# A hybrid decoder layer on one core: two small matmul runs of a key head put into one run on four array quarters, and all scores of a query block put into one run

## The chip, the cores and the metric

The kernel runs on one core of one Trainium2 chip. The metric is the device time of one execution in microseconds (us), given as the median over runs. TensorE (PE) does the matmuls, VectorE (DVE) and ScalarE (ACT) the elementwise work, GpSimd (POOL) the masks, and SyncE (SP) issues nearly all DMAs from one queue, in order.

## The reference, cut to what matters

One decoder layer over 512 tokens of width 2048 in float32. A normalised input is multiplied by one wide matrix (`w_in`); its columns feed two branches. One is sliding-window attention with 32 query heads over 4 key/value heads. The other is a gated delta rule with 16 key heads, each serving two value heads. Both are projected, gated, summed and projected again.

```
# attention, per block of 128 queries, two blocks of 128 keys in view
s = jnp.einsum('bnqhgd,bnkhd->bnhgqk', qb, kb) * (SWA_HEAD_DIM ** -0.5)
...
# delta rule, per chunk of 64 tokens
L = jnp.where(strict, jnp.einsum('bhncd,bhnsd->bhncs', k_beta, k) * decay, 0.0)
t_inv = lax.linalg.triangular_solve(eye + L, ...)
u = t_inv @ v_beta
w = t_inv @ (k_beta * jnp.exp(g)[..., None])
```

The kernel joins two chunks of 64 into one of 128. The inverse of the joined 128x128 lower triangular block is made of the two 64x64 inverses T1 and T2 and of an off-diagonal block, which is T2 times the block of L between the chunks times T1. These are the two "block products" of the title: the first multiplies the block between the chunks with T1 (its result is called `Y`), the second multiplies `Y` with T2. Both work on 64x64 matrices, for two value heads and four chunk pairs in each key head: eight matmuls each, which the profile counts as 16, since a plain float32 matmul is recorded as two.

## The kernel before, in words

Nearly all PE time goes into large products. `channel_tile` makes one tile of 128 channels by 512 tokens out of 16 steps over the 2048 inputs. Each step is three matmuls of 128x128 by 128x512 (`mm3`, lines 273 to 275), since weights and activations are split into a high and a low part: weights by ACT (`whi`, line 61) and DVE (`wlo`, line 62), half a tile at a time, into a ring of three halves. So one half serves 24 matmuls.

All the small work of the branches is written as Python generators. After every second step `channel_tile` calls `pump`, which lets each live generator go on if the number of pumps that it yielded has passed. One pump is thus six large matmuls. A generator's `yield 2` leaves 12 of them on PE between the code ahead of it and the code behind it. The tile framework then orders the instructions of each engine; it can move an instruction by a few places, and PE executes in the resulting order. PE is never left without work by intent: the small matmuls stand in the stream of large ones.

The stages follow one another: start and key heads (`delta_keys`), attention (about 540 to 1014 us), delta heads (about 1014 to 2130 us), and the output projections.

In the delta heads, `heads(wk, g)` runs for g = 0 to 15: a query tile, two value tiles and two gate tiles. `queries` loads what `keys` and `solve` left in DRAM: `ta` (T1), `lab` (the block between the chunks), `ts1` and the tiles `TT` (T2 and the full inverse to be completed). Then come, two pumps apart, `pqk`, the first block product `py` (line 955) with its copy `Y` (line 957), and the second block product `pu` (lines 961 and 962), which DVE multiplies into `TT` (line 964). The scan over the four chunk pairs reads `TT` afterwards. A 64x64 matmul uses a quarter of the array: the half of the rows that its operands' partitions name and the half of the columns that its output's partitions name. `py` uses two quarters, low rows into high columns and high rows into low columns; `pu` uses two as well, low and high rows, both into the low columns.

In attention, `group` runs for n = 0 to 3 (a key/value head with its eight query heads), and `attend` goes over four query blocks. A block's scores are made in two parts (`pp` = 0 and 1, four heads each): matmuls `S` (line 1461 in block 0, line 1466 in the others, on all four quarters), eviction by ACT (line 1473) or DVE (lines 1475, 1479), maxima (line 1484), `yield 2`. Then follow softmax, transposes `pP` and products `O` (line 1529). `scales` of the next group (`qss`, `pss`) falls into a group's last block.

PSUM has eight banks. In attention the pools hold 2 (large products), 2 (`ptp`), 3 (`psS`, the scores) and 1 (`psO`, the output `O`). In the delta heads they hold 2, 3 (`ptp`) and 3 (the scan).

Of the kernel before, what the change touches and what calls it, by code (L numbers as in the profile page):

```python
# [7 lines left out]
F32 = mybir.dt.float32  # L8
# [5 lines left out]
PSUM = bass.MemoryType.PSUM  # L14
DRAM = bass.MemoryType.DRAM

P = 128
# [3 lines left out]
NTB = T // P  # L21
EPS = 1e-6
KH = 16
VH = 32
QH = 32
HD = 64
# [19 lines left out]
class Layer:  # L46
# [653 lines left out]
    def delta_heads(self):  # L700
        tc, nc = self.tc, self.nc
        with ExitStack() as sb:
            self.ptp = sb.enter_context(tc.tile_pool(name="ptph", bufs=3, space=PSUM, reuse_waits="tile"))
            self.psc = sb.enter_context(tc.tile_pool(name="psch", bufs=3, space=PSUM, reuse_waits="tile"))
            self.gwk = sb.enter_context(tc.tile_pool(name="gwkh", bufs=1, reuse_waits="tile"))
            wk = sb.enter_context(tc.tile_pool(name="dnB", bufs=2, reuse_waits="tile"))
            self.tt = []
            for n in range(4):
                t = wk.tile([P, NTB, P], F32, tag=f"tt{n}", name=f"tt{n}", bufs=1)
                nc.gpsimd.memset(t[HD:P, :, 0:HD], 0.0)  # L710
                self.tt.append(t)
            while not self.solved:
                self.step_slow(self.solves)
            ws = sb.enter_context(tc.tile_pool(name="wsum", bufs=1, reuse_waits="tile"))
            sums = None
            for g in range(KH):
                if g == 3:
                    sums = self.paced(self.weight_sums(ws), 2.0)
                if g == 8:
                    self.drain_slow(self.solves)  # L720
                self.heads(wk, g)
            for j in range(9, 12):
                self.merge_gate("ma", j, self.ma_d)
            self.drain_live()
            self.drain_slow(sums)
# [83 lines left out]
    def solve(self, wk, b, eng):  # L809
# [48 lines left out]
        for k2 in range(2):  # L858
# [2 lines left out]
                out=self.ts_d[b, k2].rearrange("h c j i -> (h c) (j i)"), in_=A[s].rearrange("u j i -> u (j i)")  # L861
            )

    def heads(self, wk, g):

        st = {"z": []}
        self.go(self.queries(wk, g, self.channel_tile(f"q{g}"), st), 0)
        for e in range(2):
            self.go(self.values(wk, g, e, self.channel_tile(f"v{2 * g + e}"), st), 0)
        for e in range(2):  # L870
            self.go(self.zgate(wk, self.channel_tile(f"z{2 * g + e}"), st), 0)
# [23 lines left out]
    def queries(self, wk, g, ps, st):  # L895

        nc = self.nc
        sl = lambda c: slice(c * P, (c + 1) * P)
        q = wk.tile([P, T], F32, tag="y", name="yq", bufs=3)
        yield from self.conv(wk, ps, g, q)  # L900
        M = [self.decay_load(wk, 2 * g + e) for e in range(2)]
        kT = wk.tile([P, T], F32, tag="kT", name="kT")
        nc.sync.dma_start(out=kT, in_=self.kT_d[g])
        yield 2
        pt = self.ptp.tile([P, T], F32, tag="tp", name="ptq")
        self.transpose4(pt, lambda c: q[:, sl(c)])
        ss = self.sumsq(wk, pt)
        yield 3
        epsq = wk.tile([P, NTB], F32, tag="epsq", name="epsq")
        nc.vector.tensor_scalar(out=epsq, in0=ss, scalar1=EPS, scalar2=EPS * P, op0=ALU.add, op1=ALU.mult)  # L910
        yield 1
        for e in range(2):
            self.decay_mask(M[e])
        masks = self.last_mask
        ta = wk.tile([P, NTB, HD], F32, tag="ta", name="ta", bufs=1)
        lab = wk.tile([P, NTB, HD], F32, tag="lab", name="lab", bufs=1)
        ts1 = wk.tile([P, NTB, HD], F32, tag="ts1", name="ts1", bufs=1)
        qd, TT = [], []
        for e in range(2):
            h = 2 * g + e  # L920
            qe = wk.tile([P, NTB, P], F32, tag="qe", name="qe", bufs=2)
            nc.sync.dma_start(out=qe.rearrange("p c i -> p (c i)"), in_=self.eg_rows[h].partition_broadcast(P))
            qd.append(qe)
            b, hl = h // 16, h % 16
            t = self.tt[h % 4]
            for k2 in range(2):
                s = slice(k2 * HD, (k2 + 1) * HD)
                nc.sync.dma_start(out=t[s, :, s], in_=self.ts_d[b, k2, hl].rearrange("c j i -> j c i"))
            s = slice(e * HD, (e + 1) * HD)
            nc.sync.dma_start(out=ta[s], in_=self.ta_d[b, hl].rearrange("c i j -> i c j"))  # L930
            nc.sync.dma_start(out=lab[s], in_=self.lab_d[h])
            if e:
                nc.sync.dma_start(out=ts1[0:HD], in_=self.ts_d[b, 1, hl].rearrange("c j i -> j c i"))
            TT.append(t)
        yield 3
        for e in range(2):
            self.decay_exp(M[e], 2 * g + e)
        k = wk.tile([P, NTB, P], F32, tag="k", name="k")
        nc.sync.dma_start(out=k.rearrange("p c d -> p (c d)"), in_=self.k_d[g])
        yield 1  # L940
        for e in range(2):
            qf = qd[e].rearrange("p c i -> p (c i)")
            self.behind(nc.gpsimd.tensor_tensor(out=qf, in0=qf, in1=q, op=ALU.mult), masks)  # L943
        yield 1
        pqk = self.ptp.tile([P, NTB, P], F32, tag="tp", name="pqk")
        for c in range(NTB):
            nc.tensor.matmul(pqk[:, c, :], lhsT=kT[:, sl(c)], rhs=q[:, sl(c)], start=True, stop=True)
        for e in range(2):
            nc.vector.tensor_tensor(out=M[e], in0=pqk, in1=M[e], op=ALU.mult)
        yield 2  # L950
        py = self.ptp.tile([P, NTB, HD], F32, tag="tp", name="py")
        own = [slice(0, HD), slice(HD, P)]
        for c in range(NTB):
            for e in range(2):
                nc.tensor.matmul(py[own[1 - e], c, :], lhsT=lab[own[e], c, :], rhs=ta[own[e], c, :], start=True, stop=True)
        Y = wk.tile([P, NTB, HD], F32, tag="Y", name="Y", bufs=1)
        nc.vector.tensor_copy(out=Y, in_=py)
        yield 2
        pu = [self.ptp.tile([P, NTB, HD], F32, tag="tp", name="pu") for _ in range(2)]
        for c in range(NTB):  # L960
            nc.tensor.matmul(pu[0][0:HD, c, :], lhsT=Y[HD:P, c, :], rhs=TT[0][HD:P, c, HD:P], start=True, stop=True)
            nc.tensor.matmul(pu[1][0:HD, c, :], lhsT=Y[0:HD, c, :], rhs=ts1[0:HD, c, :], start=True, stop=True)
        for e in range(2):
            nc.vector.tensor_tensor(
                out=TT[e][0:HD, :, HD:P],
                in0=pu[e][0:HD],
                in1=self.neg_beta[0:HD, :, 2 * g + e].unsqueeze(2).to_broadcast([HD, NTB, HD]),
                op=ALU.mult,
            )
        yield 2  # L970
        while "v1" not in st:
            yield 1
        yield 2
        yield from self.scan(wk, g, k, kT, TT, qd, M, epsq, st)
# [338 lines left out]
    def attention(self):  # L1313
        tc, nc, a = self.tc, self.nc, self.a
        with ExitStack() as es:
            self.ptp = es.enter_context(tc.tile_pool(name="ptpa", bufs=2, space=PSUM, reuse_waits="tile"))
            self.psS = es.enter_context(tc.tile_pool(name="pS", bufs=3, space=PSUM, reuse_waits="tile"))
            self.gwk = es.enter_context(tc.tile_pool(name="gwka", bufs=1, reuse_waits="tile"))
            self.psO = es.enter_context(tc.tile_pool(name="pO", bufs=1, space=PSUM, reuse_waits="tile"))
            keep = es.enter_context(tc.tile_pool(name="akeep", bufs=1, reuse_waits="tile"))  # L1320
            self.vtok_a = keep.tile([P, NTB, 256], F32, name="vtok_a")
            self.vdiff = []
# [10 lines left out]
            blk = keep.tile([P, P], F32, name="blk")  # L1333
# [17 lines left out]
            wk = es.enter_context(tc.tile_pool(name="awk", bufs=2, reuse_waits="tile"))  # L1351
# [89 lines left out]
    def attend(self, wk, kd, n, mask, sink, qs, rs, sg, done):  # L1441
        nc = self.nc
        for i in range(NTB):
# [1 line left out]
            isl = slice(i * P, (i + 1) * P)  # L1445
            r = rs[:, i, :]
            mx = wk.tile([P, 8], F32, tag="mx", name="mx")
            sm = {}
            for pp in range(2):
                tl = []  # L1450
                for e in range(2):
                    ps = self.psS.tile([P, 2, 2 * P], F32, tag="S", name="S")
                    t = wk.tile([P, 4, P], F32, tag="sm", name="sm", bufs=5)[:, 0:2, :]
                    tl.append((ps, t))
                for j in range(2):
                    for e, (ps, t) in enumerate(tl):
                        b = slice(e * HD, (e + 1) * HD)
# [5 lines left out]
                        for u in range(2):  # L1463
# [3 lines left out]
                                ps[rr, j, HD - o : 256 - o], lhsT=q[b, i * P + o : i * P + o + HD],  # L1467
                                rhs=kd[b, (i - 1) * P + o : (i - 1) * P + o + 192], start=True, stop=True,
                            )
                wide = [P, 2, P]  # L1470
                for e, (ps, t) in enumerate(tl):
                    if i:
                        nc.scalar.copy(out=t, in_=ps[:, :, HD : HD + P])
# [46 lines left out]
                    else:  # L1520
                        nc.vector.tensor_copy(out=pT, in_=pt)
            yield 3 if i else 2
            po = self.psO.tile([P, 4, P], F32, tag="O", name="O")
            h = n % 2 * HD
            own = self.vtok_a[:, i, n * HD : (n + 1) * HD]
            for kb in kbs:
# [295 lines left out]
```

## Time and profile before

| | |
|---|---|
| median of 3 runs | 2826.55 us (2824.06 to 2827.06) |
| profiled execution | 2822.3 us, its span 2820.5 us |
| PE busy | 2790.0 us (99% of the span) |
| DVE busy | 1947.0 us (69%) |
| ACT busy | 1207.8 us (43%) |
| granted TensorE clock | 0.999 |
| attention, 540 to 1014 us | PE 472.84, DVE 340.12, ACT 214.01 us |
| delta heads, 1014 to 2130 us | PE 1111.11, DVE 735.00, ACT 451.95 us |

PE is busy nearly throughout, so a stretch of PE's time that goes away comes off the total unless another engine then makes PE wait. The ends of matmuls are modelled in the profile; what a small run costs is best read from the starts of the large matmuls around it.

### The profile page before, as it was taken

Reading aid. Unit: us, or ns where it says so; the run is one execution under the profiler, and the core shown is the slowest. Engines: PE = TensorE matmul, PEld = TensorE weight load, DVE = VectorE, ACT = ScalarE, POOL = GpSimd, SP = SyncE. Lnnn points to the kernel's source line nnn. Section 1 sums busy time; section 2 is a strip of 40 time slices with the busy share of each in tenths; the row PEclk is TensorE's granted clock in tenths of the full one; section 3 lists DMA queues with packets and bytes.
Section 4 is the critical chain, followed back from the end, with each engine's and each line's share of the span. In section 5 each row is a group of like instructions: output and inputs, shape, how many; then the busy total and the mean of one; then the engine's idle time right before and its main releaser. Section 6 shows DMA issues by size and latency. Waiting matters only on the chain.

```text
span 2820.5 us, 38292 instructions
## 1 busy us (share of the span) xinstructions
PE 2790.0 (99%) x14090; PEld 2271.8 (81%) x14090; DVE 1947.0 (69%) x3237; ACT 1207.8 (43%) x2508; POOL 145.1 (5%) x124
## 2 busy tenths in 40 slices
PE   8999999999999999999999999999999999999999
PEld 5788888877777788888888888888888788888887
DVE  7866976877758667687676666666657766664666
ACT  5554443244544434334543434434335454432443
POOL 0010110100000010000000000000000000000000
PEclk9999999999999999999999999999999999999999
DMA  9878763323262253366786666676657887885684
GB/s 403 350 241 250 257 226 129 111 79 105 74 172 92 90 183 116 113 222 228 251 262 236 225 234 245 223 241 218 228 184 243 298 301 243 300 270 186 245 313 170
DMA packets 228992, 603.38 MB, mean 214 GB/s; under 512 B 76706, under 2 KB 103074, under 8 KB 188482
## 3 DMA queue, kind: packets, MB, share of 16 engines
q1 hardware_dynamic: 228804, 600.93, 62.3%
q8 instruction: 111, 1.82, 0.3%
q14 instruction: 77, 0.63, 0.1%
HBM read 480.38 MB, written 118.24 MB: 212 GB/s over the span
## 4 chain that ended last, share of the span: by engine, by line
PE 90%; DMA 4%; DVE 3%; ACT 1%; issue 1%; SPq 0%; POOL 0%; DVEq 0%; POOLq 0%; ACTq 0%
PE mm L273 22%; PE mm L275 22%; PE mm L274 21%; PE m L274 4%; PE m L275 4%; PE m L273 4%; PE pv L996 1%; PE pod L1015 1%; PE O L1529 1%; DMA E<-g_rows 1%; PE pod L1014 1%; PE pod L1011 1%; PE pp L986 1%; PE S L1466 1%; DVE wlo L62 1%
## 5 line engine op out<-in xcount | busy, mean ns | idle before, releaser
L273 PE MATMUL mm<-hh,whi 128*128 128x512 f32 x2784 | 1127.7, 405 | 0.1
L275 PE MATMUL mm<-hh,wlo 128*128 128x512 f32 x2784 | 1088.7, 391 | 0.0
L274 PE MATMUL mm<-hl,whi 128*128 128x512 f32 x2784 | 1086.8, 390 | 0.0
L62 DVE TENSOR_TENSOR wlo<-raw,whi 128x1024 fp32r<-128x1024 f32 x516 | 634.8, 1232 | 413.4 <-ACT whi L61 403.7
L61 ACT CAST whi<-raw 128x1024 fp32r<-128x1024 f32 x516 | 540.8, 1049 | 830.2 <-PE mm L274 590.3
L273 PEld LDWEIGHTS mm<-hh,whi 128*128 128x128 f32 x2784 | 523.3, 188 | 116.8 <-issue 14.3
L275 PEld LDWEIGHTS mm<-hh,wlo 128*128 128x128 f32 x2784 | 522.5, 188 | 113.4 <-DVE wlo L62 0.3
L274 PEld LDWEIGHTS mm<-hl,whi 128*128 128x128 f32 x2784 | 524.0, 188 | 101.2 <-issue 1.4
L1261 DVE TENSOR_TENSOR q<-q,q 128x1024 f32<-128x1024 f32 x96 | 123.5, 1286 | 0.0
L807 ACT ACTIVATE E<-E,neg_g 128x128 f32<-128x128 f32 x256 | 81.0, 390 | 82.3 <-POOL E L801 80.4
L837 DVE TENSOR_TENSOR atmp<-A 128x62 f32<-128x62 f32 (+30 forms) x124 | 109.0, 879 | 0.5
L845 DVE TENSOR_TENSOR A<-A,atmp 128x62 f32<-128x62 f32 (+30 forms) x124 | 106.9, 862 | 0.5
L943 POOL TENSOR_TENSOR qe<-qe,yq 128x512 f32<-128x512 f32 x32 | 51.8, 1636 | 931.6 <-DMA qe<-eg_rows 624.2
L1016 ACT COPY osb<-pod 128x256 f32<-128x256 f32 x64 | 23.8, 372 | 153.4 <-PE pod L1015 153.4
L801 POOL TENSOR_SCALAR_AFFINE_SELECT E<-E 128x512 f32<-128x512 f32 x64 | 63.3, 1002 | 416.3 <-DMA E<-g_rows 344.2
L998 ACT COPY vn<-pv 128x256 f32<-128x256 f32 x64 | 23.9, 373 | 115.2 <-PE pv L996 115.2
L652 DVE SCALAR_TENSOR_TENSOR yv<-mm,convh,yv 128x511 f32<-128x511 f32 (+2 forms) x96 | 71.3, 743 | 1.1
L1497 ACT ACTIVATE sm<-sm,mx,rs 128x128 f32<-128x128 f32 x128 | 61.5, 482 | 2.4 <-DVE nbet L828 0.7
L1003 DVE TENSOR_SCALAR vs<-vn,kd 128x128 f32<-128x128 f32 x96 | 23.2, 284 | 54.3 <-ACT vn L998 54.3
L472 DVE SCALAR_TENSOR_TENSOR wa<-wa,silu_cb 128x2048 f32<-128x2048 f32 x22 | 50.2, 2287 | 3.7 <-DMA wa<-in_w_ada_ss 3.7
L1026 DVE SCALAR_TENSOR_TENSOR S<-S,egl,pod 128x128 f32<-128x128 f32 x64 | 19.2, 342 | 47.9 <-ACT junk L1019 47.9
L657 ACT ACTIVATE th<-yv 128x512 f32<-128x512 f32 x32 | 20.1, 629 | 65.4 <-DVE yv L652 65.4
(448 smaller groups left out, 3660.1 us busy)
## 6 DMA issues: line engine op xcount, KB each, us to landing
raw<-in_w_ch SPq DMA_DIRECT2D x158, 1024.0 KB
wa<-in_w_ada_ss SPq DMA_DIRECT2D x32, 1024.0 KB
q<-in_w_od SPq DMA_DIRECT2D x64, 512.0 KB
g_d<-q SPq DMA_DIRECT2D x64, 512.0 KB
raw<-g_d SPq DMA_DIRECT2D x32, 1024.0 KB
raw<-in_w_od SPq DMA_DIRECT2D x24, 1024.0 KB
gw<-in_w_ada_gate SPq DMA_DIRECT2D x16, 1024.0 KB
E<-g_rows SPq DMA_DIRECT2D x64, 256.0 KB
```

The costliest lines, as they stand in the source:

```text
L61: h = self.nc.scalar.copy(out=hi, in_=src)
L62: l = self.nc.vector.tensor_tensor(out=lo, in0=src, in1=hi.bitcast(F32), op=ALU.subtract)
L273: nc.tensor.matmul(ps, lhsT=wh, rhs=xh, start=first, stop=False)
L274: nc.tensor.matmul(ps, lhsT=wh, rhs=xl, start=False, stop=False)
L275: self.last_mm = nc.tensor.matmul(ps, lhsT=wl, rhs=xh, start=False, stop=last)
L652: nc.vector.scalar_tensor_tensor(out=y[:, s:], in0=ps[:, : T - s], scalar=w[:, j : j + 1], in1=y[:, s:], op0=ALU.mult, op1=ALU.add)
L801: self.last_mask = self.nc.gpsimd.affine_select(out=E, in_=E, pattern=[[0, NTB], [1, P]], compare_op=ALU.is_ge, fill=NEG, base=0, channel_ ...
L807: self.nc.scalar.activation(E[:, c, :], E[:, c, :], AF.Exp, bias=self.neg_g[:, c, h : h + 1])
L837: eng.tensor_tensor(out=t, in0=A[:, m : m + 1, m + 1 :].to_broadcast([P, m, n]), in1=A[:, :m, m : m + 1].to_broadcast([P, m, n]), op=ALU.mult,
L845: self.behind(eng.tensor_tensor(out=A[:, :m, m + 1 :], in0=A[:, :m, m + 1 :], in1=t, op=ALU.add))
L1261: self.behind(nc.vector.tensor_tensor(out=q[f], in0=q[x], in1=q[y], op=ALU.add))
L1497: nc.scalar.activation(t, t, AF.Exp, scale=r[:, h : h + 1], bias=mx[:, h : h + 1], accum_out=den[:, h : h + 1])
```

## The change

In the delta heads, the first block product of key head g+1 is now made in the run of the second block product of key head g. It writes the upper partitions of the two `pu` banks, so that the run uses all four quarters: `pu` of g the low columns, the first product of g+1 the high columns. `Y` is then copied by DVE in two pieces and waits for a whole key head until it is read. `ta` and `lab` are loaded one key head ahead, behind the loads of `TT` and `ts1`. For g = 0 a generator of its own (`first_blocks`) loads them and makes the first product six pumps into the stage. The inverses of the second half of the heads are now asked for at g = 7 instead of 8.

In attention, both parts' score matmuls stand ahead of the evictions, so that there are 16 matmuls in a row (8 in block 0) in place of twice 8 (twice 4). The scores get a fourth PSUM bank; the bank of `O` is given up and `O` takes turns with `pP`, `qss` and `pss` in `ptp`.

```
-                if g == 8:
+                if g == 7:
                     self.drain_slow(self.solves)
...
+    def block_product(self, pu, blk, c):
+        ta, lab = blk
+        for e in range(2):
+            own = slice(e * HD, (e + 1) * HD)
+            self.nc.tensor.matmul(pu[1 - e][HD:P, c, :], lhsT=lab[own, c, :], rhs=ta[own, c, :], start=True, stop=True)
+    def block_copy(self, wk, pu):
+        Y = self.Y = wk.tile([P, NTB, HD], F32, tag="Y", name="Y", bufs=1)
+        self.nc.vector.tensor_copy(out=Y[HD:P], in_=pu[1][HD:P])
+        self.nc.vector.tensor_copy(out=Y[0:HD], in_=pu[0][HD:P])
+    def first_blocks(self, wk):
+        blk = self.block_load(wk, 0)
+        yield 6
+        pu = [self.ptp.tile([P, NTB, HD], F32, tag="tp", name="pu") for _ in range(2)]
+        for c in range(NTB):
+            self.block_product(pu, blk, c)
+        self.block_copy(wk, pu)
...
+        while self.Y is None:
+            yield 1
+        Y = self.Y
+        blk = self.block_load(wk, g + 1) if g + 1 < KH else None
...
-        yield 2
-        py = self.ptp.tile([P, NTB, HD], F32, tag="tp", name="py")
...
-        nc.vector.tensor_copy(out=Y, in_=py)
-        yield 2
+        yield 4
         pu = [self.ptp.tile([P, NTB, HD], F32, tag="tp", name="pu") for _ in range(2)]
         for c in range(NTB):
             nc.tensor.matmul(pu[0][0:HD, c, :], lhsT=Y[HD:P, c, :], rhs=TT[0][HD:P, c, HD:P], start=True, stop=True)
             nc.tensor.matmul(pu[1][0:HD, c, :], lhsT=Y[0:HD, c, :], rhs=ts1[0:HD, c, :], start=True, stop=True)
+            if blk:
+                self.block_product(pu, blk, c)
...
+        if blk:
+            self.block_copy(wk, pu)
...
-            self.psS = es.enter_context(tc.tile_pool(name="pS", bufs=3, space=PSUM, reuse_waits="tile"))
+            self.psS = es.enter_context(tc.tile_pool(name="pS", bufs=4, space=PSUM, reuse_waits="tile"))
-            self.psO = es.enter_context(tc.tile_pool(name="pO", bufs=1, space=PSUM, reuse_waits="tile"))
...
-                wide = [P, 2, P]
+            wide = [P, 2, P]
+            for pp, tl in enumerate(tiles):
                 for e, (ps, t) in enumerate(tl):
                     if i:
                         nc.scalar.copy(out=t, in_=ps[:, :, HD : HD + P])
...
-            po = self.psO.tile([P, 4, P], F32, tag="O", name="O")
+            po = self.ptp.tile([P, 4, P], F32, tag="tp", name="O")
```

PE, delta heads, from `pqk` of one key head to the end of its second block product, before (between the rows shown stand 12 large matmuls each time):

```order
L947 MATMUL pqk<-yq,kT 128x128 x4
L320 MATMUL ptv<-ident,yv 128x128 x4
...
L955 MATMUL py<-ta,lab 64x64 x8
...
L961 MATMUL pu<-tt_9017,Y 64x64
L962 MATMUL pu<-ts_9782,Y 64x64
L961 MATMUL pu<-tt_9017,Y 64x64
L962 MATMUL pu<-ts_9782,Y 64x64
```

The same place now, with 24 large matmuls ahead of the run:

```order
L981 MATMUL pqk<-yq,kT 128x128 x4
L320 MATMUL ptv<-ident,yv 128x128 x4
...
L987 MATMUL pu<-tt_9013,Y 64x64
L988 MATMUL pu<-ts_9795,Y 64x64
L882 MATMUL pu<-ta,lab 64x64 x2
L987 MATMUL pu<-tt_9013,Y 64x64
L988 MATMUL pu<-ts_9795,Y 64x64
L882 MATMUL pu<-ta,lab 64x64 x2
```

The run of `py` is gone and its eight matmuls stand between those of `pu`, quarter by quarter. Key head 15 has the old `pu` run alone, and one run of eight `pu<-ta,lab` stands in the query tile of key head 0: 17 runs instead of 32.

PE, attention, the end of the third group (n = 2, blocks 2 and 3, with `qss` of the next group), before; large matmuls between the rows are left out:

```order
L1466 MATMUL S<-kd_4496,aq 64x192 x8
...
L1466 MATMUL S<-kd_4496,aq 64x192 x8
...
L320 MATMUL pP<-ident,sm 128x128
...
L320 MATMUL pP<-ident,sm 128x128 x3
...
L1466 MATMUL S<-kd_4496,aq 64x192 x8
...
L1466 MATMUL S<-kd_4496,aq 64x192 x8
L1427 MATMUL qss<-qsq,blk 32x128 x16
```

And now:

```order
L1496 MATMUL S<-kd_4493,aq 64x192 x16
...
L1496 MATMUL S<-kd_4493,aq 64x192 x11
...
L320 MATMUL pP<-ident,sm 128x128 x8
...
L1496 MATMUL S<-kd_4493,aq 64x192 x5
...
L1456 MATMUL qss<-qsq,blk 32x128 x3
...
L1456 MATMUL qss<-qsq,blk 32x128 x13
```

In most blocks the two runs of eight become one of 16, as in the first row. At a group's end the second score run had no large matmuls between itself and `qss`; now `qss` stands alone, and in groups 0 and 2 it is cut in two by two large matmuls. In group 2 alone, block 3's scores are cut in 11 and 5, while the transposes `pP`, which were strewn over five large matmuls, stand together. From block 2's last score run to its first transpose there were 57 large matmuls; from its one score run to the transposes there are 66. Of the 391 runs of other matmuls in the stream of large ones, 362 are left.

DVE, attention, the evictions of one block's scores (second block of the first group), before:

```order
L1479 COPY_PREDICATED sm<-other,S 64x2x64 x3
L1484 TENSOR_REDUCE mx<-sm 128x2
L1479 COPY_PREDICATED sm<-other,S 64x2x64
L1484 TENSOR_REDUCE mx<-sm 128x2
L62 TENSOR_TENSOR wlo<-raw,whi 128x1024
```

And now:

```order
L1510 COPY_PREDICATED sm<-other,S 64x2x64 x3
L1515 TENSOR_REDUCE mx<-sm 128x2
L1510 COPY_PREDICATED sm<-other,S 64x2x64 x2
L1515 TENSOR_REDUCE mx<-sm 128x2
L1510 COPY_PREDICATED sm<-other,S 64x2x64 x2
L1515 TENSOR_REDUCE mx<-sm 128x2
L1510 COPY_PREDICATED sm<-other,S 64x2x64
L1515 TENSOR_REDUCE mx<-sm 128x2
L62 TENSOR_TENSOR wlo<-raw,whi 128x1024
```

The low half of the next weights now stands behind all 12 evictions and maxima of a block; before, it stood between the first six and the last six.

More of the change, by code (lines that the diff above doesn't have):

```diff
@@ L713, in delta_heads @@
                 self.step_slow(self.solves)
+            self.Y = None
+            self.go(self.first_blocks(wk), 1)
             ws = sb.enter_context(tc.tile_pool(name="wsum", bufs=1, reuse_waits="tile"))
@@ L862, in solve, with block_load @@
             )
+    def block_load(self, wk, g):
+        ta = wk.tile([P, NTB, HD], F32, tag="ta", name="ta", bufs=1)
+        lab = wk.tile([P, NTB, HD], F32, tag="lab", name="lab", bufs=1)
+        for e in range(2):
+            h = 2 * g + e
+            s = slice(e * HD, (e + 1) * HD)
+            self.nc.sync.dma_start(out=ta[s], in_=self.ta_d[h // 16, h % 16].rearrange("c i j -> i c j"))
+            self.nc.sync.dma_start(out=lab[s], in_=self.lab_d[h])
+        return ta, lab
+    def block_product(self, pu, blk, c):
+        ta, lab = blk
+        for e in range(2):
+            own = slice(e * HD, (e + 1) * HD)
[11 more added lines that the diff above has]
+        self.block_copy(wk, pu)
     def heads(self, wk, g):
@@ L914, in queries @@
         masks = self.last_mask
-        ta = wk.tile([P, NTB, HD], F32, tag="ta", name="ta", bufs=1)
-        lab = wk.tile([P, NTB, HD], F32, tag="lab", name="lab", bufs=1)
         ts1 = wk.tile([P, NTB, HD], F32, tag="ts1", name="ts1", bufs=1)
@@ L928, in queries @@
                 nc.sync.dma_start(out=t[s, :, s], in_=self.ts_d[b, k2, hl].rearrange("c j i -> j c i"))
-            s = slice(e * HD, (e + 1) * HD)
-            nc.sync.dma_start(out=ta[s], in_=self.ta_d[b, hl].rearrange("c i j -> i c j"))
-            nc.sync.dma_start(out=lab[s], in_=self.lab_d[h])
             if e:
@@ L949, in queries @@
             nc.vector.tensor_tensor(out=M[e], in0=pqk, in1=M[e], op=ALU.mult)
-        yield 2
-        py = self.ptp.tile([P, NTB, HD], F32, tag="tp", name="py")
[L952 to L957, printed above, removed]
-        yield 2
+        yield 4
         pu = [self.ptp.tile([P, NTB, HD], F32, tag="tp", name="pu") for _ in range(2)]
@@ L1447, in attend @@
             mx = wk.tile([P, 8], F32, tag="mx", name="mx")
-            sm = {}
+            sm, tiles = {}, []
             for pp in range(2):
@@ L1454, in attend @@
                     tl.append((ps, t))
+                tiles.append(tl)
                 for j in range(2):
```

## Prediction

> **What bounds the kernel now.** I read the page first: busy times, then the chain that ended last.
>
> ```profile
> PE 2790.0 (99%) x14090; PEld 2271.8 (81%) x14090; DVE 1947.0 (69%) x3237; ACT 1207.8 (43%) x2508; POOL 145.1 (5%) x124
> ...
> PE 90%; DMA 4%; DVE 3%; ACT 1%; issue 1%; SPq 0%; POOL 0%; DVEq 0%; POOLq 0%; ACTq 0%
> ```
>
> And the view of the cores:
>
> ```profile
> core 0: 2820.5 us, clock 0.999
> ```
>
> PE is busy for 99% of the span and is 90% of the chain. So the question is how much of PE's time the change takes away, and whether another engine then makes PE wait. Busy time can't price a small run, since overlapping matmuls hide in it; I price a run by how far it pushes the large matmuls apart. The timeline of PE at key head 0's two block products:
>
> ```profile
> 1047.90 0.39 PE L275 MATMUL mm<-hh,wlo 128*128 128x512 f32 x1
> 1048.22 0.68 PE L955 MATMUL py<-ta,lab 64*64 64x64 f32 x16
> ...
> 1049.17 0.39 PE L274 MATMUL mm<-hl,whi 128*128 128x512 f32 x1
> ...
> 1051.46 0.39 PE L275 MATMUL mm<-hh,wlo 128*128 128x512 f32 x1
> 1051.78 0.27 PE L961 MATMUL pu<-tt,Y 64*64 64x64 f32 x1
> ...
> 1051.94 0.22 PE L961 MATMUL pu<-tt,Y 64*64 64x64 f32 x1
> 1051.95 0.22 PE L962 MATMUL pu<-ts,Y 64*64 64x64 f32 x1
> 1052.00 0.22 PE L961 MATMUL pu<-tt,Y 64*64 64x64 f32 x1
> ...
> 1052.73 0.39 PE L274 MATMUL mm<-hl,whi 128*128 128x512 f32 x1
> ```
>
> From 1049.17 to 1051.46 there are ten undisturbed steps of large matmuls: 0.229 us each. Around a small run the first large matmul behind it starts late and the second is back in step, so I take the second. Around `py`: 1047.90 to 1049.17 is 1.27, less two steps is 0.81 us. Around `pu`: 1051.46 to 1052.73, again 0.81. Inside `pu` the two quarters (lines 961 and 962) start within 0.01 of each other, and one quarter's next matmul follows 0.06 later. Eight matmuls to a quarter are 0.46; the other 0.35 is the price of leaving the large stream and coming back.
>
> **Four quarters at once.** Block products use two. The scores use four, so their rows show whether four run side by side. The first fence is the timeline at one score run; the two lines behind it are the same run cut off by narrow windows, so that the count grows by one round of four:
>
> ```profile
> 599.88 0.39 PE L275 MATMUL mm<-hh,wlo 128*128 128x512 f32 x1
> 600.20 0.88 PE L1466 MATMUL S<-kd,aq 64*64 64x192 f32 x16
> ...
> 601.35 0.40 PE L274 MATMUL mm<-hl,whi 128*128 128x512 f32 x1
> ```
>
> ```profile
> 600.20 0.56 PE L1466 MATMUL S<-kd,aq 64*64 64x192 f32 x8
> 600.20 0.72 PE L1466 MATMUL S<-kd,aq 64*64 64x192 f32 x12
> ```
>
> Every four more matmuls, one to a quarter, lengthen the run by 0.16 us, which is three times the 0.06 of a 64-column matmul for 192 columns: four quarters cost what one costs. The run costs 601.35 - 599.88 - 0.46 = 1.01 us; four rounds are 0.65, and 0.36 is leaving and coming back, as for `pu`.
>
> **The change part by part.** *Key heads.* Of 32 runs (16 `py`, 16 `pu`) 17 are left: 15 merged ones, key head 15's `pu`, and one `py`-like run for key head 0. A merged run has 8 matmuls in each of four quarters. If they run side by side, it costs what `pu` costs, 0.81, and some 0.01 for two more starts. Taken away: 15 x 0.81 = 12.2, less 15 x 0.01 = 0.2, so 12.0 us. The trace has no 64-column run on four quarters. Bounds: nothing shared at all gives 12.2; if the two quarters of one row half take turns, a merged run costs 0.35 + 2 x 0.46 = 1.27 and 15 x (1.62 - 1.27) = 5.3 us go. I take 12.0, since the score rows are the nearest: same quarters, same kind of matmul, only wider.
>
> A rule of the Trainium skill speaks against this. "TensorE: Matmul & The Clock Gate", part 3 (what overlaps and what doesn't), says that a weight load overlaps running matmuls only where the row group differs. In a merged run two quarters always share their rows; by that rule they would take turns, and the sum would hold 5.3 for the key heads. The score run, where pairs of quarters share rows too, does not bear it out: 0.16 us to a round of four.
>
> *Attention.* Thirteen of the 32 score runs vanish into a neighbour: blocks 0, 1 and 2 of all groups and block 3 of the last. Each takes its 0.36 along: 4.7 us (block 0's runs use row halves; I price them alike). At the ends of groups 0 to 2 nothing is saved, since the second score run had shared its way out and back with `qss`, which now stands alone. Cuts cost one more way out and back each: `qss` in groups 0 and 2, the scores in group 2: -3 x 0.36 = -1.1. In group 2 the strewn transposes stand together. There and in an ordinary block the timeline has:
>
> ```profile
> 856.04 0.39 PE L275 MATMUL mm<-hh,wlo 128*128 128x512 f32 x1
> 856.81 0.33 PE L320 MATMUL pP<-ident,sm 128*128 128x128 f32 x1 [0.38 <-DVE sm L1505]
> ...
> 860.32 0.39 PE L273 MATMUL mm<-hh,whi 128*128 128x512 f32 x1
> ```
>
> ```profile
> 616.90 0.39 PE L275 MATMUL mm<-hh,wlo 128*128 128x512 f32 x1
> 617.13 1.03 PE L320 MATMUL pP<-ident,sm 128*128 128x128 f32 x8
> ...
> 618.24 0.39 PE L274 MATMUL mm<-hl,whi 128*128 128x512 f32 x1
> ```
>
> Strewn, the eight cost 4.28 less seven steps (1.60), 2.7 us with their waits for DVE; together, 1.34 - 0.46 = 0.9. Now 66 large matmuls stand between the scores and them instead of 57, which is 2 us more for DVE, so I count the full 1.8. Attention: 4.7 - 1.1 + 1.8 = 5.4 us.
>
> *The wait for `Y`, the loads, DVE.* These views (waits of PE, ACT and SP, and groups of DVE and ACT) price the rest:
>
> ```profile
> PE pu L961 <- DVE Y L957: 0.8, 1, 0.8
> ACT whi L61 <- PE mm L274: 590.3, 226, 6.5
> SPq L930 <- PE py L955: 35.8, 11, 7.2
> L957 DVE COPY Y<-py x16: 408/416/425, 1048.9 to 2063.5; 128x256 f32<-128x256 f32 x16
> L964 DVE TENSOR_TENSOR tt<-pu,neg_beta x32: 403/407/417, 1053.9 to 2068.4; 64x256 f32<-64x256 f32 x32
> L1479 DVE COPY_PREDICATED sm<-other,S 64x128 f32<-64x128 int32 x96 | 28.9, 301 | 12.8 <-ACT sm L1473 11.3
> L1484 DVE TENSOR_REDUCE mx<-sm 128x2 f32<-128x256 f32 x64 | 25.9, 411 | 0.6
> L62 DVE TENSOR_TENSOR wlo<-raw,whi 128x1024 fp32r<-128x1024 f32 x516 | 634.8, 1232 | 413.4 <-ACT whi L61 403.7
> L61 ACT CAST whi<-raw 128x1024 fp32r<-128x1024 f32 x516 | 540.8, 1049 | 830.2 <-PE mm L274 590.3
> ```
>
> PE waited once, 0.8 us, for `Y`; it is now ready a key head ahead: 0.8 saved. Two copies of 64 partitions (by line 964, 0.41 each) replace one of 0.42: 16 x 0.4 = 6.6 us more on DVE, hidden as long as DVE (69% busy) has room; the scan reads `TT` 42 large matmuls (9.6 us) behind the run, and the four DVE pieces take 1.6. Of that cover nothing is used up.
>
> SP waited for `py` before it could overwrite `ta` (line 930), and behind that queue the weights wait. Now `ts1` and then `ta` wait for the merged run, where `ts1` had waited for `pu` already; so SP is free at the same point, and only the four small issues come behind it. At g = 0 four loads go ahead of the other loads of the stage, each some half a microsecond; nothing there is read for tens of microseconds. The second solve is all written in the order ahead of key head 7, so asking for it a key head earlier moves nothing. `O` in `ptp` waits for nothing new: it needs both `pT` copies as operands anyway, and these free the banks.
>
> Sum: 12.0 + 5.4 + 0.8 = 18.2 us. The profiled execution was 2822.3 us, its span 2820.5; it becomes 2804.1. The median of the runs shown lies 4.2 above the profiled one, so 2826.55 - 18.2 = 2808.3 us, 0.64% faster.
>
> **The rivals.** *The quarters of one row half take turns.* For it: no run here has four 64-column quarters, and 32 starts in 0.46 us is denser than any run shown. Against it: the score rounds and the 0.01 between two starts of `pu`. It gives 5.3 + 5.4 + 0.8 = 11.5, so 2815 us.
>
> *Attention gives nothing.* The order there is fragile: the framework already cut scores and `qss` anew in two groups, and DVE, which made PE wait for transposes at 856, gets its work in thicker bursts. If waits eat the 5.4, it is 12.0 + 0.8, so 2813.8 us.
>
> *Slower: the low halves come late.* All 12 evictions and maxima of a block, 8 x 0.30 + 4 x 0.41 = 4.0 us, now stand ahead of `wlo`, where six (2.0) stood. ACT starts a cast as soon as PE frees one of three halves (226 waits of that kind), two halves or 48 steps ahead of need: 11.0 us, less 1.05 and 1.23 for the two splits leaves 8.7. The extra 2.0 fits in. It decides only where the room is already down below 2.0 in most blocks; to turn 18.2 into a loss PE would have to wait over 1.1 us in all of the 16 blocks. At the worst, no room anywhere, 16 x 2.0 = 32 us: 14 us slower, 2840 us. Against it: the list of PE's waits has none of `mm` for `wlo`.
>
> **How the numbers follow.** Forecast 0.74, turns 0.11, attention eaten 0.09, late halves 0.06. Runs of one kernel here spread over 3 us (0.1%), and 0.2% (5.7 us) is about what a measurement can tell from no change. The forecast itself reaches from 2804 to 2812; the range, 2803 to 2817, adds both milder rivals. Faster holds the first three cases but for 0.02: 0.92. The last case is half a wash and half a loss: same 0.05, slower 0.03.
>
> **What would show it.** Right: a timeline at a merged run where 32 matmuls push the second large matmul by 0.82, no `py`, and score runs of 32 pushing by 1.66. Wrong: a merged run of 1.27, matmuls of one row half following each other; new waits of PE for `wlo`, `O` or `sm` in attention; SP waiting at the loads of `ta` so long that weights come late.

## The result and the profile after

The changed kernel takes 2809.93 us (median of 6 runs, 2807.83 to 2813.47), the kernel before on the same chip 2825.31 (6 runs, 2822.64 to 2827.09). The ratio is 0.9947, its 95% interval 0.9934 to 0.996: 15.4 us or 0.5% faster. Forecast were 2808.3 us and a gain of 18.2. The profiled executions differ by 13.1 us: 2822.3 and 2809.24, with spans of 2820.5 and 2807.4.

The page of the changed kernel, busy times and the shares of the chain that ended last:

```profile
PE 2777.5 (99%) x14090; PEld 2271.1 (81%) x14090; DVE 1951.0 (69%) x3253; ACT 1207.4 (43%) x2508; POOL 144.3 (5%) x124
...
PE 89%; DMA 4%; DVE 3%; issue 1%; ACT 1%; POOL 0%; SPq 0%; DVEq 0%; POOLq 0%; ACTq 0%
```

PE still sets the time, with as many matmuls as before. It is busy for 12.5 us less, and the span is 13.1 us shorter: the time went out of what small runs take from the stream of large matmuls. Key head 0's merged run in PE's timeline (start, duration, operation):

```profile
1050.53 0.39 PE L275 MATMUL mm<-hh,wlo 128*128 128x512 f32 x1
1050.85 0.27 PE L987 MATMUL pu<-tt,Y 64*64 64x64 f32 x1
1050.85 0.27 PE L988 MATMUL pu<-ts,Y 64*64 64x64 f32 x1
1050.86 0.27 PE L882 MATMUL pu<-ta,lab 64*64 64x64 f32 x2
...
1051.32 0.23 PE L882 MATMUL pu<-ta,lab 64*64 64x64 f32 x2
1051.47 0.50 PE L273 MATMUL mm<-hh,whi 128*128 128x512 f32 x1
1051.81 0.39 PE L274 MATMUL mm<-hl,whi 128*128 128x512 f32 x1
```

All four quarters start within 0.01 us. From 1050.53 to the second large matmul behind the run are 1.28 us; less two undisturbed steps of 0.227 it is 0.82 (824 to 825 ns in all 15 merged runs). So 32 matmuls on four quarters cost nearly what 16 on two cost before (0.81). An ordinary block's score run of 32:

```profile
599.77 0.39 PE L275 MATMUL mm<-hh,wlo 128*128 128x512 f32 x1
600.09 1.53 PE L1496 MATMUL S<-kd,aq 64*64 64x192 f32 x32
601.55 0.50 PE L273 MATMUL mm<-hh,whi 128*128 128x512 f32 x1
601.89 0.40 PE L274 MATMUL mm<-hl,whi 128*128 128x512 f32 x1
```

It pushes by 2.12 - 0.46 = 1.66 us, as forecast, against twice 1.01. The list of PE's waits no longer has `Y`, and has four new entries. Two are short (`ptq` for `yq`, 0.4 us, and `O` for `pT`, 0.2); the others are (in total, times, longest):

```profile
PE mm L275 <- DVE wlo L62: 1.9, 1, 1.9
PE pp L1016 <- DVE S L1053: 1.2, 1, 1.2
```

The first stands at the end of attention's group 2, and so does the whole shortfall of attention; the second stands in the delta heads. I compare the starts of the same large matmuls `mm<-hh,whi` in all traces; in the kernel before the four that I use start at 554.04, 847.42, 894.38 and 980.37 us and bound the nine ordinary blocks of groups 0 to 2 with the turns between these groups (I), the end of group 2 with block 0 of group 3 (II), and the rest of group 3 (III).

| change of length, us | I | II | III | attention |
|---|---|---|---|---|
| forecast, from the prediction's prices | -2.9 | -1.4 | -1.1 | -5.4 |
| changed kernel | -3.0 | +2.6 | -1.1 | -1.5 |

Forecast for I: nine runs by 0.36, less the cut of `qss` in group 0. For II: block 0's run, the strewn transposes, less two cuts. Parts I and III came out as worked out. What happened in II, from the timelines of ACT, DVE and PE:

```profile
845.10 4.42 DVE L831 TENSOR_TENSOR A<-A,nbet 128x4096 f32<-128x4096 f32 x1
846.49 1.03 ACT L61 CAST whi<-raw 128x1024 fp32r<-128x1024 f32 x1
850.04 1.22 DVE L62 TENSOR_TENSOR wlo<-raw,whi 128x1024 fp32r<-128x1024 f32 x1
851.31 0.50 PE L275 MATMUL mm<-hh,wlo 128*128 128x512 f32 x1 [1.87 <-DVE wlo L62]
```

The high half was cast by 847.5, but the low half started only at 850.04: ahead of it stands a 4.42 us instruction of the second solve, whose instructions are spread over this stage. In the kernel before, that instruction came behind a low half (DVE's timeline):

```profile
846.08 1.22 DVE L62 TENSOR_TENSOR wlo<-raw,whi 128x1024 fp32r<-128x1024 f32 x1
...
848.93 4.42 DVE L829 TENSOR_TENSOR A<-A,nbet 128x4096 f32<-128x4096 f32 x1
```

DVE has hardly any slack here, by the windows view of the changed kernel (length, then busy time of PE, PEld, DVE, ACT, POOL; granted clock of PE ahead of the last two columns):

```profile
770.00:836.00 66.00, 66.00 (x327) 51.16 (x325) 34.55 (x69) 31.68 (x68) 0.00 (x0) 1.00 0.55 152
836.00:860.00 24.00, 22.13 (x135) 17.14 (x134) 22.47 (x48) 11.55 (x31) 3.87 (x3) 0.93 0.42 140
```

From 770 to 836 us DVE is busy for 52% of the time, from 836 to 860 for 94% (83% in the kernel before).

The transposes `pP` that were to come together did so, in the changed kernel:

```profile
857.85 0.40 PE L275 MATMUL mm<-hh,wlo 128*128 128x512 f32 x1
858.08 1.03 PE L320 MATMUL pP<-ident,sm 128*128 128x128 f32 x8
...
859.19 0.40 PE L274 MATMUL mm<-hl,whi 128*128 128x512 f32 x1
```

They push by 1.34 - 0.46 = 0.9 us for 2.7 before, as forecast. What part II lost is mainly the wait of 1.9 us and, right behind it, a stretch at half clock from 852.54 us that costs about 1.6 us (last section).

### The profile page after: what moved, and what is told of

The parts are those of the page before. It is cut to its first block, busy times and chain, and to the rows that moved or that the text cites. A ratio compares the mean times of both kernels' runs of the same rounds, so it can differ in the third digit from the quotient of the medians.

```text
span 2807.4 us, 38312 instructions
## 1 busy us (share of the span) xinstructions
PE 2777.5 (99%) x14090; PEld 2271.1 (81%) x14090; DVE 1951.0 (69%) x3253; ACT 1207.4 (43%) x2508; POOL 144.3 (5%) x124
## 4 chain that ended last, share of the span: by engine, by line
PE 89%; DMA 4%; DVE 3%; issue 1%; ACT 1%; POOL 0%; SPq 0%; DVEq 0%; POOLq 0%; ACTq 0%
PE mm L273 21%; PE mm L275 21%; PE mm L274 21%; PE m L274 5%; PE m L275 5%; PE m L273 5%; DMA E<-g_rows 1%; PE pv L1026 1%; PE pod L1045 1%; PE O L1560 1%; PE pod L1044 1%; PE pp L1016 1%; PE pod L1041 1%; DVE wlo L62 1%; DMA wa<-in_w_ada_ss 1%
## 5 line engine op out<-in xcount | busy, mean ns | idle before, releaser
L273 PEld LDWEIGHTS mm<-hh,whi 128*128 128x128 f32 x2784 | 524.2, 188 | 113.8 <-issue 11.8
L1045 PE MATMUL pod<-vn,E 128*128 128x128 f32 x256 | 46.8, 275 | 0.0
```

Of the source, the lines that this page charges most:

```text
L273: nc.tensor.matmul(ps, lhsT=wh, rhs=xh, start=first, stop=False)
L1045: nc.tensor.matmul(po[:, e, :], lhsT=M[e][:, c, :], rhs=vn[:, e, :], start=c == 0, stop=True)
```

## Experiments

Theory: the key heads (the merged runs, in the delta heads) gave what was forecast, and attention's shortfall is DVE's load at the end of group 2, the solve's long instruction ahead of a low half above all. Rivals: the key heads gave less and attention more; or joining the scores makes the next thing late at a group's end, whatever the solve does. All times are medians with the lowest and highest run; the kernel before had 2824.84, 2825.01 and 2824.4 in the three sets.

| kernel | us | runs | ratio to before (95%) |
|---|---|---|---|
| e1_heads | 2811.88 (2809.54 to 2813.3) | 5 | 0.9951 (0.9939 to 0.9964) |
| e2_attn | 2823.58 (2818.61 to 2827.29) | 11 | 0.9993 (0.9984 to 1.0001) |
| e3_split | 2810.96 (2809.62 to 2811.02) | 5 | 0.9949 (0.9936 to 0.9963) |
| e6_in_turn | 2812.6 (2811.48 to 2813.26) | 5 | 0.9955 (0.9942 to 0.9967) |
| a2_again | 2810.31 (2806.29 to 2813.44) | 5 | 0.9948 (0.9936 to 0.9961) |
| e4_last_apart | 2807.79 (2807.71 to 2809.08) | 5 | 0.9941 (0.9928 to 0.9953) |
| e7_later | 2808.79 (2805.19 to 2811.29) | 5 | 0.9941 (0.9927 to 0.9954) |
| e8_later_apart | 2807.6 (2806.22 to 2809.87) | 5 | 0.994 (0.9928 to 0.9952) |
| e9_group3 | 2805.38 (2803.17 to 2810.02) | 5 | 0.9936 (0.9924 to 0.9949) |
| e10_group3_apart | 2809.48 (2803.63 to 2811.85) | 5 | 0.9938 (0.9924 to 0.9951) |

Runs of one kernel spread over up to 9 us, so verdicts on single waits go by the traces, one of each kernel, with this table of attention:

| change of length, us | I | II | III | attention |
|---|---|---|---|---|
| a2_again | -3.3 | +2.1 | -1.1 | -2.3 |
| e2_attn | -3.3 | +2.2 | -1.1 | -2.3 |
| e3_split | -2.7 | -0.8 | -1.1 | -4.6 |
| e4_last_apart | -2.8 | +2.0 | -1.1 | -1.9 |
| e7_later | -2.6 | +0.8 | -1.1 | -2.9 |
| e8_later_apart | -2.8 | +2.7 | -1.1 | -1.3 |
| e9_group3 | -3.3 | -0.8 | +0.7 | -3.4 |
| e10_group3_apart | -2.4 | -1.1 | +0.8 | -2.8 |

**The key heads alone** (e1_heads: `attention` as in the kernel before, the rest as changed).

> The key-head part of the change alone; attention is as before. Theory (prices of runs add up): a merged run pushes the large matmuls apart by 0.82 us, 15 runs of 0.81 go, and the one wait for Y (0.8 us) goes: 12.8 us less than before, some 2812.5 us, about 0.9955 of before. Rival (the trace of the changed kernel gains from something else too, such as a luckier phase of waits): clearly less than 12, with merged runs that still push by 0.82.

Measured: 13.0 us less, with an interval from 10 to 17. In its trace all 15 merged runs push by 0.825, and attention is as long as before (within 0.1 us).

**Attention alone** (e2_attn: `attention` as changed, the rest as before).

> The attention part alone; the key heads are as before. Theory: as in the trace of the changed kernel, blocks 0 to 2 of the four groups save 0.34 to 0.43 us each (4.6 us), and the end of the third group loses 3.1 us again, by a 1.9 us wait of PE for a low half of the weights and 3.4 us at half clock behind it: 1.5 us less than before, some 2824 us. Rival (the loss at that place was chance of one execution): 5 us less, 2820 us, no wait there.

Measured: 1.3 us less, with an interval that takes in no change, and the wait for the low half again 1.9 us, without half clock behind it. In its trace attention shrinks by 2.3 us; but in the delta heads, which are as before, the one wait for `Y` is now 2.0 us instead of 0.8, and a stretch at half clock follows it (1594 us). So the 1.3 is not attention alone. The parts add up to 14.3 of the 15.4. The rival that the key heads gave less and attention more is out by the traces: attention gives 1.5 to 2.3 us in the four that have the whole edit of it and nothing else there (the changed kernel, a2_again, e2_attn and e6_in_turn).

**Do quarters really run side by side?** e6_in_turn issues the same 32 matmuls in another order:

```diff
-            if blk:
-                self.block_product(pu, blk, c)
+        for c in range(NTB if blk else 0):
+            self.block_product(pu, blk, c)
```

> The changed kernel, with the same 16 matmuls of a merged run in another order: first the eight of the second product (two quarters), then the eight of the next first product (the other two quarters). Theory (PE starts matmuls in order, so quarters only work side by side where their matmuls alternate): a run pushes by 0.35 + 2 x 0.46 = 1.27 us instead of 0.82, 15 x 0.45 = 6.8 us more than the changed kernel, some 2816.7 us. Rival (PE reaches past the first eight to idle quarters, or the gain is only in leaving the large stream once less): 0.82 still, some 2810 us.

PE's timeline at key head 0:

```profile
1052.33 0.39 PE L275 MATMUL mm<-hh,wlo 128*128 128x512 f32 x1
1052.64 0.27 PE L987 MATMUL pu<-tt,Y 64*64 64x64 f32 x1
...
1052.94 0.27 PE L882 MATMUL pu<-ta,lab 64*64 64x64 f32 x2
...
1053.11 0.51 PE L882 MATMUL pu<-ta,lab 64*64 64x64 f32 x11
1053.55 0.50 PE L273 MATMUL mm<-hh,whi 128*128 128x512 f32 x1
1053.89 0.39 PE L274 MATMUL mm<-hl,whi 128*128 128x512 f32 x1
```

The run pushes by 1.56 - 0.46 = 1.10 us in all 15 cases, between the 1.27 and the 0.82 that were expected. The matmuls of line 882 start at 1052.94, while those of lines 987 and 988 still run, so they overlap in part. The order inside the run is worth 0.28 us a run, 4.2 us in 15; in total this kernel is 12.2 us faster than before, where the changed one was 15.4.

**The long instruction in four pieces** (e3_split, in both solves):

```diff
-        self.behind(eng.tensor_tensor(out=A, in0=A, ...))
+        for q in range(4):
+            if q:
+                yield 1.1
+            part = A[:, 16 * q : 16 * q + 16]
+            self.behind(eng.tensor_tensor(out=part, in0=part, ...))
```

> The changed kernel, with the first product of a solve, A times nbet (one DVE instruction of 4.4 us on 128x4096), cut into four of 128x1024 with three pumps or so between them. Theory (the attention part lost its gain at the end of the third group since this long instruction stood ahead of a low half of the weights): no wait of PE for a low half there, no half clock, and 3 to 4.5 us less than the changed kernel, some 2806 us. Rival (the thicker bursts of evictions or the shared PSUM banks keep DVE late there): a wait of 1 us or more remains at that place, under 1 us less.

The wait for the low half is gone and attention shrinks by 4.6 us, the most of all runs. But the total stayed (13.9 us less than before): a miss. With the three yields the second solve's last step comes at 1378 us instead of 1344, and PE waits more in the delta heads (1000 to 1500 us; in the changed kernel 0, 2.9 and 0.4 us there, and 1.2 for `S`):

```profile
PE ptv L320 <- DVE yv L659: 4.4, 2, 2.8
PE pto L320 <- DVE osb L1079: 3.4, 2, 2.5
PE ptq L320 <- DVE yq L659: 1.2, 1, 1.2
```

That the later solve brings these waits on is not shown: in e9_group3 below the solve ends later still (1415 us), and they stay away.

**The yardstick again, and the instruction moved.** Four kernels. e7_later and e8_later_apart ask for the second solve's first work later:

```diff
-        yield 8.0
+        yield 11.0 if b == 1 else 8.0
...
-            yield 0.1 + 0.00115 * m * n
+            yield (0.1 + 0.00115 * m * n) * (0.717 if b == 1 and m < 12 else 1)
```

e4_last_apart and e8_later_apart (and e10_group3_apart below) compute block 3's scores in two parts:

```diff
+            both = i < NTB - 1 or n == 3
+            for batch in ([0, 1],) if both else ([0], [1]):
```

> The changed kernel, unaltered, as the yardstick for the three others. All theories: 15.0 us under the kernel before (its median was 15.4, its profiled pair 13.1 under), the wait of PE for the low half again 1.9 us near 851 us, since its instructions stand in the same order. Open is the clock: theory that a PE wait of about 2 us brings on a stretch of half clock only sometimes expects at least one of the two stretches (852 and 1176 us) to be missing or another in its place; the rival, that the order of the instructions fixes them, expects both again, 3.4 us long each.

14.7 us less; the wait for the low half again (1.8). As the theory of a clock that follows only sometimes expects, the stretch of half clock behind that wait is missing and another stands at 2225 us; the one near 1177 us came again. The clock is told below. Without it the transposes behind the wait come too early for DVE:

```profile
856.74 0.39 PE L275 MATMUL mm<-hh,wlo 128*128 128x512 f32 x1
856.97 0.27 PE L320 MATMUL pP<-ident,sm 128*128 128x128 f32 x1
857.73 1.44 PE L320 MATMUL pP<-ident,sm 128*128 128x128 f32 x7 [0.48 <-DVE sm L1536]
...
859.24 0.39 PE L274 MATMUL mm<-hl,whi 128*128 128x512 f32 x1
```

They push by 2.50 - 0.46 = 2.0 us here, for 0.9 in the changed kernel's first trace. So part II is 2.1 us longer than before, nearly as much as there.

> The changed kernel with the 4.42 us instruction A<-A,nbet of the second solve asked for 3 units later in its pacing, given back over the next eleven steps, so that it stands behind three low halves instead of ahead of the first, and nearly all of the later order is as it was. Theory (this instruction ahead of the low half ate the attention part): no wait for the low half, no half clock near 852 us, all 32 score matmuls of group 2's last block in one run, and from there on 3.4 us ahead of the changed kernel; 18.5 us under the kernel before. Rival (VectorE has no room in this stretch, so whatever stands behind the long instruction is late): the wait goes to O, which needs pT, up to 4.4 us, and the total stays at 15 under.

The waits of PE from 840 to 880 us in e7_later:

```profile
PE pss L1462 <- DVE ssb L1458: 1.4, 1, 1.4
PE mm L275 <- DVE wlo L62: 0.5, 1, 0.5
```

Both were half right. The wait for the low half fell from 1.9 to 0.5, and the scores stand in one run; but another wait came some 20 us on, behind the moved instruction, for `ssb` and not for `O`. Part II is 1.8 us shorter than in the changed kernel instead of 3.4, the total 16.2 less than before instead of 18.5.

> As the one before, and block 3 of groups 0 to 2 computes its scores in two parts again, so that the second part shares its run with qss. Theory (a run out of the large stream and back costs 0.36 us, and a cut qss one more): against the one before, the two cuts of qss in groups 0 and 2 go (2 x 0.36), the rest is even: 0.7 us less, 19.2 under the kernel before. Rival (the block's scores are worth joining there too, 0.36 a group): 3 x 0.36 - 0.7 = 0.4 us more, 18.1 under.

The same two waits:

```profile
PE pss L1462 <- DVE ssb L1458: 2.1, 1, 2.1
PE mm L275 <- DVE wlo L62: 0.5, 1, 0.5
```

With 2.1 us for `ssb`, and a stretch at half clock from 873.88 us behind it that costs 1.6 more, part II is no better than in the changed kernel. The cut of `qss` in group 2 is gone and worth 0.4 there, as the theory has it, but these two hide it. In the total it can't be told from e7_later.

> The changed kernel with block 3 of groups 0 to 2 in two parts again, and nothing else: the long instruction still stands ahead of the low half. Theory: the two cuts of qss go, 0.7 us less than the changed kernel, so 15.7 under the kernel before, and the wait for the low half in group 2 stays at about 1.9 us. Rival (joining block 3's scores is what made VectorE late there, since four evictions stand together): the wait shrinks below 1 us and the total is 18 under.

The wait for the low half stayed at 1.9 us, so joining block 3's scores did not bring it on. The gain forecast for the two cuts is not in attention (-1.9 against -1.5 and -2.3 of the changed kernel's two traces). The cuts do go, and at the one in group 0 the runs cost 0.4 us less, as forecast; but in group 1 there is now this:

```profile
PE O L1563 <- DVE pT L1551: 0.7, 1, 0.7
```

The total is lower than the yardstick's, with intervals that overlap; I count it as undecided.

**The solve out of group 2's end** (e9_group3; e10_group3_apart adds the edit of e4_last_apart):

```diff
-        yield 8.0
+        yield 24.0 if b == 1 else 8.0
```

> The changed kernel with the second solve's first work asked for 16 units later in its pacing and not given back, so that its 4.42 us instruction falls into an ordinary block of group 3, and group 2's end has nothing of the solve. Theory (the loss is VectorE's load at group 2's end, and the joined scores are sound): no wait of PE between 840 and 880 us above 0.5; the attention stage, from its first to its last projection, shrinks by 4.6 to 5.9 us against the kernel before instead of 1.5 to 2.3; the total is 18 us under the kernel before. Rival (joining the scores by itself makes the next thing late at a group's end): a wait for ssb, aq or a low half of over 1 us stays there without the solve, and the stage shrinks by 3 at most.

At the group's end, where the low half now starts as soon as ACT has cast the high half (the first two rows), and where the long instruction has gone (the others):

```profile
847.45 1.22 DVE L62 TENSOR_TENSOR wlo<-raw,whi 128x1024 fp32r<-128x1024 f32 x1 [2.85 <-ACT whi L61]
848.73 0.50 PE L275 MATMUL mm<-hh,wlo 128*128 128x512 f32 x1 [0.52 <-DVE wlo L62]
...
919.72 4.42 DVE L831 TENSOR_TENSOR A<-A,nbet 128x4096 f32<-128x4096 f32 x1
...
937.88 1.85 PE L320 MATMUL pP<-ident,sm 128*128 128x128 f32 x8 [0.90 <-DVE sm L1536]
```

No wait but one of 0.5 us from 820 to 900, part II 0.8 shorter than before instead of 2.6 longer: the rival, which asked for a wait of over 1 us there without the solve, is out. The 0.5 that is left comes from ACT, where the cast stands among the eight exponentials of the block. But attention shrinks by 3.4 instead of the 4.6 at least that I expected, since the instruction costs something in an ordinary block too: `pP` waits 0.9 for `sm` and then runs at DVE's pace, 1.85 us for eight transposes; part III is 1.9 longer than in the changed kernel. The total is 19.0 less than before, expected 18: the lowest median of all, 4.9 us below the yardstick's, though their intervals overlap. That the total came out as expected is luck: in its trace attention gives only 1.1 to 1.9 us more than in the changed kernel's two, and the delta heads (1014 to 2130 us) 3.2 to 3.6 more, since neither the half clock near 1177 us nor the wait of `pp` for `S` is there.

> As the one before, and block 3 of groups 0 to 2 computes its scores in two parts again. Theory (each cut of qss costs a way out and back): the cuts in groups 0 and 2 are gone, so the attention stage shrinks by 0.7 more, 5.3 to 6.6; 18.7 us under the kernel before. Rival (a joined block 3 is worth as much as any other, 0.36 a group): the stage shrinks 0.4 less than in the one before.

Attention shrinks by 0.6 less than in the one before, not 0.7 more: part II wins 0.3, by the cut in group 2, and part I loses 0.9, where `O` now waits twice for `pT`, 1.0 us in all. The theory that only the cuts count fell; the rival's 0.4 less is nearer, but most of the loss is these waits. By the medians too there is nothing to win.

## Why the prediction came out as it did

The time was in the range, and 3 us of the forecast gain were missing. That it is no more is partly luck of the runs: in the changed kernel's two traces attention and the delta heads (1014 to 2130 us) together give 11.8 and 13.0 us, where 18.2 were forecast for them.

- *Key heads, 12.0, and the wait for `Y`, 0.8: right.* A merged run costs 0.825 us where 0.82 was forecast. By the starts of the large matmuls all runs of block products together, with the wait for `Y`, push by 27.0 us in the kernel before and by 14.0 now: 13.0 for 12.8. That the median of e1_heads has 13.0 too is partly luck, given its interval. The price taken from the score rows, four quarters cost what one does, holds for 64 columns as for 192.
- *Nothing else in the delta heads: wrong.* The stage as a whole shrinks by 10.3 and 10.7 us in the changed kernel's two traces and by 11.7 in e1_heads. A stretch at half clock takes 1.3 to 1.7 us in each, behind a wait that the kernel before has as well, and the new wait of `pp` for `S` takes 0.9 to 1.2. The prediction had no term for either. What makes `S` late is open; `pp` waits in seven of the ten traces with merged runs and in neither of the two without.
- *The rival of turns: refuted,* by the same 0.825 against its 1.27. So the rule of the Trainium skill that was weighed there ("TensorE: Matmul & The Clock Gate", part 3) is not borne out by the merged run either, while e6_in_turn shows that the order in the queue decides how much of it overlaps.
- *Attention, 5.4: mis-sized.* It measured 1.5 and 2.3 in the changed kernel's two traces and 2.3 in e2_attn's. The price of a run out and back, 0.36, was right in parts I and III (-3.0 and -1.1 for -2.9 and -1.1). The step that failed is that of group 2's end, where the prediction counted 1.8 for the transposes and put new waits at nothing. DVE had more time ahead of the transposes, but in the new order the solve's long instruction stands ahead of the low half, and PE waits 1.9 us for it. Behind that wait either the clock halves (1.6 us) and the transposes give their 1.8, or it doesn't and they give 0.7. The rival that attention gives nothing, because waits eat its gain, came nearest: waits and half clock ate 3 to 4 of the 5.4.
- *The rival of late low halves: right in its mechanism, at one place,* for 1.9 us. It set the 2.0 us that more evictions and maxima take against 8.7 us of room in an ordinary block, and against it spoke that no `mm` had waited for `wlo`. Neither took in what else DVE holds at that place: a single instruction of 4.4 us. Where that instruction is away (e9_group3) part II shrinks by 0.8 of the 1.4 forecast.
- *A cut of a run, 0.36: right as a price, too crude as a forecast.* Where a cut goes, the runs cost 0.3 to 0.4 us less (e4_last_apart in group 0, e8_later_apart and e10_group3_apart in group 2); but waits for `pT` take their place. A price for a run holds only while nothing waits behind it.
- *DVE's 6.6 us more for `Y` and SP's queue at nothing: not contradicted.* The two copies take 0.43 each, 7.0 us more in all; no merged run is pushed apart by a wait in the changed kernel, and PE's list of waits has none for a load.

Still open is a rest of the total: by its two traces the changed kernel lies 8.9 to 13.1 us ahead of the kernel before at the last large matmul of `mm`, and the stage behind the delta heads, which the change does not touch, is 1.6 us shorter than there in the one and 3.0 longer in the other.

## What to carry to other kernels

Price a small run by what it pushes the large stream apart, and join runs that use different quarters, alternating the quarters in the queue: here that was worth 0.8 us for each pair of block products and 0.36 for each pair of score runs, wherever nothing waited behind. Where the change re-orders another engine, list that engine's longest single instructions near each place and ask what each now stands ahead of; an average of 69% says nothing about 24 us at 94%. An instruction that is moved out of the way takes its cost along, so look where it lands.

## What the runs showed of the hardware

**Half clock comes on a fixed grid.** The same 2.2 us wait of `pto` for `osb` near 1176 us left the clock alone in the kernel before and halved it in the changed one. Two windows of 3.41 us each, the kernel before first, then the changed kernel twice:

```profile
1172.78:1176.19 3.41, 2.47 (x11) 1.70 (x10) 3.24 (x8) 3.40 (x9) 0.03 (x1) 1.00 0.00 0
1176.19:1179.61 3.42, 2.11 (x14) 1.91 (x15) 3.42 (x6) 0.00 (x0) 0.00 (x0) 1.00 0.54 137
```

```profile
1173.40:1176.81 3.41, 1.17 (x9) 1.01 (x9) 3.24 (x6) 1.05 (x3) 0.00 (x0) 1.00 0.14 29
1176.81:1180.22 3.41, 3.41 (x11) 2.73 (x10) 1.75 (x3) 0.00 (x0) 0.00 (x0) 0.50 0.91 372
```

```profile
849.13:852.54 3.41, 1.54 (x11) 1.03 (x6) 3.41 (x7) 3.04 (x5) 0.00 (x0) 1.00 0.04 7
852.54:855.96 3.42, 3.42 (x9) 2.69 (x9) 3.42 (x7) 0.00 (x0) 1.28 (x1) 0.50 0.52 125
```

Within a trace the changes of the granted clock lie whole multiples of 3.4133 us apart (in the changed kernel 852.54 and 1176.81 by 95 of them; all twelve traces agree), and from 100 us on half clock lasts one such window. In the kernel before, a window's edge falls into the wait and PE is busy for over 2 us in either window; in the changed kernel one window holds the wait, PE is busy in it for 1.17 us, and the next window runs at half clock. In the twelve traces, from 100 to 2700 us: after a window in which PE was idle for 1.87 us or more, by the profile's busy time, the next was at half clock in 13 of 13 cases, between 1.75 and 1.84 in 2 of 5, with less never. The Trainium skill, "TensorE: Matmul & The Clock Gate", part 1 (the clock gate), tells of a free-running window of 4096 cycles, about 3.4 us, and of half rate after an idle window; the traces agree on the length, and show that 1.9 us of idleness in a window are enough. The grid stands elsewhere against the kernel's start in every trace (in the kernel before an edge lies at 1176.19 us, in the changed one at 1176.81). That may be one reason why runs of one kernel spread; it is not shown. The theory for a2_again called it chance; the rows fit a rule with a chance phase.

**Half clock costs little where another engine sets the pace, and its full price where not.** In the changed kernel the stretch from 852.54 takes large matmuls from 0.23 to 0.43 us a step, about 1.6 us in all. Yet part II is 2.6 longer with it and 2.1 longer in a2_again, which has the wait without it: there PE reached the transposes earlier and waited for DVE, and they cost 2.0 us instead of 0.9. In e8_later_apart the stretch from 873.88 costs 1.6 us too, and nothing behind it in part II comes cheaper than in e7_later, which has none there.
